# Seven-product down projections for the first parts of all half layers

## The chip, the cores and the metric

The kernel runs on one core of a Trainium2 chip. A core has TensorE (PE in the profile; its weight loads are listed as PEld), VectorE (DVE), ScalarE (ACT), GpSimd (POOL) and SyncE (SP); the last three also issue DMAs, and DMAs that add to their destination go through POOL's queue. The metric is the device time of one execution in microseconds, lower is better; shown is the median of the runs of a kernel.

## The reference

One inference step of a decoder with two layers on 512 prompt positions and 8 sample positions, 1024 channels. Each layer does x += 0.5 * SwiGLU(rms(x)), then a mixer, then a second half SwiGLU. So there are four "half layers" with their own weights:

```python
def _swiglu(x, wg, wu, wd):
    return (jax.nn.silu(x @ wg) * (x @ wu)) @ wd
...
x = x + 0.5 * _swiglu(_rmsnorm(x, norm_g[l, 0]), ffn_w_gate[l, 0], ffn_w_up[l, 0], ffn_w_down[l, 0])
```

`wg` and `wu` are 1024 x 2816, `wd` is 2816 x 1024. The mixer of layer 0 is a causal pooling over windows of 2 to 16 positions, that of layer 1 a windowed attention with sinks; neither is touched by the change. Outputs are the two final activations and the states.

## The kernel before

All activations lie transposed, channels on partitions, in tiles of 128 x 520: the 520 columns are the tokens (512 and 8), and they are worked in two halves of `H` = 260. Every float32 product is made of three products of float32r operands: a tensor is split into a high part (a rounded copy, made by ScalarE, names ending in `h`) and a low part (the rest, made by VectorE, names ending in `l`), and high x high, low x high and high x low are added in PSUM (`terms`). Weights are split the same way into `wh` (L260) and `wl` (L261), in pieces of 128 x 4 x 128, from loaded chunks `raw`.

A half layer (`ffn`, index `fi` from 0 to 3) has 22 tiles of 128 hidden channels, cut into `PARTS` of 8, 8 and 6. For each part it first makes the hidden tiles (gate and up products, silu, their product), then the down projection of that part, which is added to x.

- **Hidden tiles.** The first `NPL[fi]` (4, 3, 2, 3) tiles of a half layer are plain (`plain_tile`): they need only x, since the sums of inputs for the other form are being made meanwhile (`sums`, L783 to L791, fed in by `hooks`), and the norm factor R is not known yet. All others use a seven-product form (`strassen_tile`): gate and up, upper and lower half of the channels, and the two halves of the tokens make 2 x 2 blocks, and seven products of sums of blocks replace eight. The sums on the side of x are the tiles `tt` (names `th`, `tl`). The sums on the side of the weights are made by accumulating DMAs on POOL's queue (L191, L192) and by VectorE (L197, L201); the tile `S` has four buffers.
- **Which operands are free.** The plain tiles read both token halves of all tiles of x (`mov`). The seven-product tiles don't read the second token half of the first four.
- **Down projection.** In the plain form (L815 to L851) each of 8 output tiles takes its 8 or 6 hidden tiles times three terms times two token halves. In the seven-product form (`strassen_down`, L718) pairs of output tiles are made of seven products; it wants sums of hidden tiles, which `HiddenSums` makes as the hidden tiles come: for every two of them B11 (a split of half a tile), T1, T2, B21, B22, T3 and T4. B11 is put where it needs no room of its own: in the second token half of `mov[k]` (L606), which nobody reads any more. Before the change only the second part of each half layer is in `SEVEN` (L33) and has this form; the others use `Hidden`, one split for each hidden tile.

`Weights` holds the order of chunks and pieces: `plan_ffn` writes for each part which chunks are loaded and which pieces are split, in the order of use, and up to five pieces (`ahead`) are split before TensorE gets to them. Chunks have three buffers. A scheduler that simulates the program with its own costs orders the instructions of each engine, except where `later` pins them; so a change in one place can move instructions of all engines nearby. PSUM is handed out in four pairs of banks (`duo`), so that two seven-product tiles can be under way.

At the end of a part in seven-product form its last product is left open and is made inside the next tile (`unfinished`, `finish`).

Of the kernel before, what the change touches and what calls it, by code (L numbers as in the profile page):

```python
# [11 lines left out]
F32 = mybir.dt.float32  # L12
F32R = mybir.dt.float32r
I32 = mybir.dt.int32
AF = mybir.ActivationFunctionType
ALU = mybir.AluOpType
AX = mybir.AxisListType

P = 128
# [5 lines left out]
TOK = SP + NS  # L25
# [4 lines left out]

FIRST = 264
NPL = (4, 3, 2, 3)
SEVEN = {(0, 1), (1, 1), (2, 1), (3, 1)}  # L33
HD = 64
NB = SP // P
WINS = (2, 4, 8, 16)
# [244 lines left out]
def yoco_step(ctx, tc, ins, outs):  # L281
    nc = tc.nc
# [3 lines left out]
    V, S, T = nc.vector, nc.scalar, nc.tensor  # L286
# [16 lines left out]
    def pair(tags, shape, dtype=F32R):  # L303

        return tuple(big.tile(shape, dtype, tag=t, name=t) for t in tags)
# [9 lines left out]
    def split(dst, src, scale=None):  # L315

        hi, lo = dst
        if scale is None:
            S.activation(hi, src, AF.Copy)  # L319
            V.tensor_tensor(lo, src, hi.bitcast(F32), op=ALU.subtract)  # L320
        else:
            S.activation(hi, src, AF.Copy, scale=scale)
            V.scalar_tensor_tensor(lo, src, scale, hi.bitcast(F32), op0=ALU.mult, op1=ALU.subtract)
# [9 lines left out]
    def ld(dst, src):  # L333
        return lambda raw: later(nc.sync.dma_start(dst(raw), src))
# [22 lines left out]
    def plan_ffn(l, f):  # L357
# [4 lines left out]
        for pi, n in enumerate(PARTS):  # L362
            for j in range(t0, t0 + n):
# [13 lines left out]
                else:  # L377
                    W.sums(ch, ld(lambda t: t, u3[:, :4, c]))
            if (2 * l + f, pi) in SEVEN:
                tiles = []  # L380
# [36 lines left out]
    for t in range(0, 8, 2):  # L417
        gp, i = t // 4, t % 4
# [3 lines left out]
                    lambda raw, e=e: raw.rearrange("p k (e i d) -> p k e i d", e=2, i=2)[:, :, e],  # L422
# [12 lines left out]
    for g in range(2):  # L435
        for c in range(2):
# [4 lines left out]
                        lambda raw, e=e: half(raw)[e * 64 : (e + 1) * 64],  # L441
# [28 lines left out]
    def hcols(t, hf):  # L470
        return t[:, hf * H : (hf + 1) * H]
# [14 lines left out]
    nu = [2]  # L486
# [88 lines left out]
    class Hidden(list):  # L575


        def __init__(self, tags):
            self.tags = tags

        def take(self, g):
            hp = pair(self.tags, [P, TOK])
            split(hp, g)
            self.append(hp)

    class HiddenSums:


        def __init__(self, tmp, mov, tags, n):
            self.tmp, self.mov, self.tags, self.n = tmp, mov, tags, n  # L590
            self.b = {q: [] for q in ("B11", "T1", "T2", "B21", "B22", "T3", "T4")}
            self.even = None

# [9 lines left out]
        def take(self, g):  # L603
            k = len(self.b["T3"])
            if self.even is None:
                b11 = tuple(hcols(z, 1) for z in self.mov[k])  # L606
                split(b11, hcols(g, 0))
                self.b["B11"].append(b11)
                t12 = self.tmp.tile([P, TOK], F32, tag="u", name="t12", bufs=nu[0])
                t1 = hcols(t12, 0)  # L610
                V.tensor_tensor(t1, hcols(g, 0), hcols(g, 1), op=ALU.subtract)
                z = pair(self.tags, [P, TOK])
                self.both(z, "T1", "T2")
                if 2 * k + 2 == self.n:
                    split(tuple(hcols(a, 0) for a in z), t1)
                self.even = g, t12, z
                return
            (e, t12, z), self.even = self.even, None
            t1, t2 = hcols(t12, 0), hcols(t12, 1)
            t34 = self.tmp.tile([P, TOK], F32, tag="u", name="t34", bufs=nu[0])  # L620
            t3, t4 = hcols(t34, 0), hcols(t34, 1)
            V.scalar_tensor_tensor(t2, t1, -1.0, hcols(g, 1), op0=ALU.mult, op1=ALU.subtract)
            if 2 * k + 2 == self.n:
                split(tuple(hcols(a, 1) for a in z), t2)
            else:
                split(z, t12)
            w = pair(self.tags, [P, TOK])
            self.both(w, "B21", "B22")
            split(w, g)
            V.tensor_tensor(t3, hcols(g, 1), hcols(e, 1), op=ALU.subtract)  # L630
            V.scalar_tensor_tensor(t4, t2, -1.0, hcols(g, 0), op0=ALU.mult, op1=ALU.subtract)
            v = self.more(k)
            self.both(v, "T3", "T4")
            split(v, t34)
# [159 lines left out]
    def ffn(fi, tmp, mov, hooks, tt, tags, after, before_last=None, first=None, by_parts=None, hold=False):  # L794

        j = 0
        for pi, n in enumerate(PARTS):
            last = pi == len(PARTS) - 1
            seven = (fi, pi) in SEVEN
            hs = HiddenSums(tmp, mov, tags, n) if seven else Hidden(tags)  # L800
            for _ in range(n):
                if j == 0 and first is not None:
                    plain_end(tmp, *first, hs)
# [90 lines left out]
    with ff_pool() as tmp:  # L894
# [132 lines left out]

        after = deferred(1, tmp, "g", XX, mov1, TW, True)
        ffn(0, tmp, mov0, start_hooks(tmp, 0, tt, 2), tt, HH, after, pool_prep(), first, hold=True)

    with tc.tile_pool(name="pm", bufs=2, reuse_waits="tile") as pm:
# [133 lines left out]
    with ff_pool() as tmp:  # L1165
# [112 lines left out]
        step = lambda: next(steps, None)  # L1278
        hooks = [step, outputs] + [step] * 4
        ffn(2, tmp, mov3, hooks, tt, XX, deferred(4, tmp, "g", HH, mov4), attention_prep())  # L1280


# [586 lines left out]
```

## Time and profile before

| | us |
|---|---|
| median of 3 runs (lowest, highest) | 1665.18 (1664.43, 1668.25) |
| the profiled execution | 1663.9 |
| its span, from first to last instruction | 1661.8 |
| TensorE busy | 1633.8 (98% of the span) |
| VectorE busy | 1329.6 (80%) |
| ScalarE busy | 931.6 (56%) |
| POOL busy | 196.5 (12%) |
| mean granted TensorE clock | 0.995 |

How to read the rows: L with a number is a line of the kernel. "ps<-th,wh" says that the tile ps is written from th and wh. In groups, "x704 | 469.2, 688 | 127.4 <-ACT wh L260 125.1" means 704 instructions, 469.2 us busy, 688 ns mean of one, 127.4 us idle time of the engine before them, most of it ended by ScalarE's instruction on L260 that writes wh. In a timeline the columns are start, duration, engine, line, operation, tiles, shapes; idle time before it stands in brackets. In a list of waits the numbers are total us, times, longest. Instructions of one engine overlap a little: a VectorE instruction of 0.70 us can be followed by the next 0.60 us after its start, and busy time counts the overlap once.

The half layers begin (first matmuls of the first part) at about 9, 403, 794 and 1294 us; their second parts run from 151.7 to 270.3, 539.2 to 657.6, 913.3 to 1031.7 and 1429.2 to 1547.9.

### The profile page before, as it was taken

The page shows a single profiled execution, that of the slowest core. Times are in us where ns is not written, and L with a number is a line of the kernel's source. Part 1 is how long each engine was busy: PE and PEld are TensorE (multiplying, and loading weights), DVE is VectorE, ACT ScalarE, POOL GpSimd, SP SyncE. Part 2 cuts the span into 40 slices and gives each one's busy share as a digit, 9 for nine tenths or more (in the row PEclk, how much of TensorE's full clock was granted, in tenths as well). Part 3 has the DMA queues.
Part 4 walks back from the last instruction along what each step waited for, and adds up shares of the span by engine and source line. Part 5 has one row for each costly group of instructions (what it writes and reads, how often), then busy time and mean ns, then how long its engine had stood idle before and what let it go on. Part 6 is the DMA issues. An engine that isn't in the chain of part 4 may idle for free.

```text
span 1661.8 us, 34718 instructions
## 1 busy us (share of the span) xinstructions
PE 1633.8 (98%) x13578; PEld 1621.9 (98%) x13578; DVE 1329.6 (80%) x2589; ACT 931.6 (56%) x1900; POOL 196.5 (12%) x262
## 2 busy tenths in 40 slices
PE   9999999999999999999999999999989999999997
PEld 9999999999999999999999999999989999999996
DVE  6866999877875899888775899886787785799876
ACT  5643665556652665555552665555785653465554
POOL 0101111000101111100201111101210100111100
PEclk9999999999999999999999999999999999999999
DMA  8545778752555778744756787753222555577741
GB/s 222 124 136 130 174 178 180 183 157 91 123 157 134 165 176 180 165 134 107 185 149 134 162 178 182 166 179 97 57 52 77 134 139 141 131 176 181 176 130 52
DMA packets 345712, 240.69 MB, mean 145 GB/s; under 512 B 11438, under 2 KB 316326, under 8 KB 345508
## 3 DMA queue, kind: packets, MB, share of 16 engines
q1 hardware_dynamic: 313790, 183.10, 39.7%
q0 software_dynamic: 28000, 50.28, 18.6%
q10 hardware_dynamic: 3758, 5.09, 1.0%
q8 instruction: 107, 1.75, 0.5%
q14 instruction: 57, 0.47, 0.1%
HBM read 185.56 MB, written 6.11 MB: 115 GB/s over the span
## 4 chain that ended last, share of the span: by engine, by line
PE 92%; ACT 3%; DVE 2%; issue 1%; DMA 1%; POOL 0%; ACTq 0%; DVEq 0%; POOLq 0%
PE ps L563 55%; PE ps L535 31%; DMA pr<-in_bands_dram 1%; PE ps L1077 1%; PE ps L1455 1%; ACT sm L1399 1%; PE ps L1052 0%; PE ps L1424 0%; ACT xh L319 0%; PE ps L494 0%; PE ps L1743 0%; DVE wl L261 0%; PE ps L1368 0%; ACT wh L260 0%; PE ps L932 0%
## 5 line engine op out<-in xcount | busy, mean ns | idle before, releaser
L260 ACT ACTIVATE wh<-raw 128x512 fp32r<-128x512 f32 (+1 forms) x762 | 452.0, 620 | 394.1 <-PE ps L535 197.4
L261 DVE TENSOR_TENSOR wl<-raw,wh 128x512 fp32r<-128x512 f32 (+1 forms) x762 | 501.0, 678 | 136.4 <-ACT wh L260 133.7
L563 PE MATMUL ps<-th,wh 128*128 128x260 f32 x1216 | 344.0, 284 | 1.2 <-ACT sa L701 0.9
L563 PE MATMUL ps<-tl,wh 128*128 128x260 f32 x1216 | 342.6, 282 | 0.0
L563 PE MATMUL ps<-th,wl 128*128 128x260 f32 x1216 | 341.2, 283 | 0.2 <-DVE wl L261 0.2
L563 PEld LDWEIGHTS ps<-th,wh 128*128 128x128 f32 x1216 | 228.7, 188 | 2.8 <-ACT sa L701 1.1
L563 PEld LDWEIGHTS ps<-tl,wh 128*128 128x128 f32 x1216 | 229.0, 188 | 0.0
L563 PEld LDWEIGHTS ps<-th,wl 128*128 128x128 f32 x1216 | 227.9, 188 | 0.4 <-DVE wl L261 0.4
L563 PE MATMUL ps<-xh,wh 128*128 128x260 f32 x784 | 220.9, 283 | 0.7 <-ACT sb L698 0.7
L563 PE MATMUL ps<-xl,wh 128*128 128x260 f32 x784 | 220.3, 282 | 0.0
L563 PE MATMUL ps<-xh,wl 128*128 128x260 f32 x784 | 218.7, 282 | 0.0
L192 POOL DMA_DIRECT2D raw<-raw x92 | 79.3, 862 | 1148.1 <-DVE wl L261 421.1
L535 PE MATMUL ps<-hh,wh 128*128 128x260 f32 x956 | 193.4, 284 | 0.6 <-ACT vtok L1236 0.6
L535 PE MATMUL ps<-hl,wh 128*128 128x260 f32 x956 | 193.2, 282 | 0.0
L535 PE MATMUL ps<-hh,wl 128*128 128x260 f32 x956 | 192.1, 282 | 0.0
L563 PEld LDWEIGHTS ps<-xh,wh 128*128 128x128 f32 x784 | 147.3, 188 | 1.3 <-ACT sb L698 1.3
L535 PEld LDWEIGHTS ps<-hh,wh 128*128 128x128 f32 x956 | 146.8, 188 | 1.5 <-ACT vtok L1236 0.9
L535 PEld LDWEIGHTS ps<-hl,wh 128*128 128x128 f32 x956 | 147.7, 188 | 0.0
L563 PEld LDWEIGHTS ps<-xl,wh 128*128 128x128 f32 x784 | 147.5, 188 | 0.0
L535 PEld LDWEIGHTS ps<-hh,wl 128*128 128x128 f32 x956 | 147.3, 188 | 0.0
L563 PEld LDWEIGHTS ps<-xh,wl 128*128 128x128 f32 x784 | 146.9, 189 | 0.0
L563 PE MATMUL ps<-hl,wh 128*128 128x260 f32 x448 | 125.8, 282 | 0.0
(329 smaller groups left out, 3391.1 us busy)
## 6 DMA issues: line engine op xcount, KB each, us to landing
raw<-in_ffn_w_gate_dram SPq DMA_DIRECT2D x87, 512.0 KB, 4.6
raw<-in_ffn_w_up_dram SPq DMA_DIRECT2D x87, 512.0 KB, 5.8
raw<-raw POOLq DMA_DIRECT2D x92, 256.0 KB, 3.4
S<-raw POOLq DMA_DIRECT2D x92, 256.0 KB, 4.5
S<-in_ffn_w_up_dram SPq DMA_DIRECT2D x76, 256.0 KB, 5.6
raw<-in_ffn_w_down_dram SPq DMA_DIRECT2D x16, 1024.0 KB, 5.4
raw<-in_ffn_w_down_dram SPq DMA_DIRECT2D x64, 256.0 KB, 4.6
raw<-in_ffn_w_down_dram SPq DMA_DIRECT2D x16, 768.0 KB, 4.3
```

The lines of the kernel that those rows point to most:

```text
L192: G.dma_start(blk(raw, 2, 1), blk(raw, 1, 1), accum_op=ALU.add)
L260: pin(nc.scalar.activation(dh, src, AF.Copy))
L261: pin(nc.vector.tensor_tensor(dl, src, dh.bitcast(F32), op=ALU.subtract))
L535: ins = T.matmul(banks[:, hf, :H], a[:, kk, :], hcols(b, hf), start=(first and i == 0), stop=(last and i == 2),)
L563: T.matmul(bank[:, :H], a[:, kk, :], b, start=(not more and kk == 0 and i == 0), stop=(kk == 3 and i == 2), skip_group_check=more,)
L1077: T.matmul(po[:, half * 256 : half * 256 + 256], z[:, tau, c], b, start=(i == 0), stop=(i == len(lst) - 1),)
L1399: S.activation(z, z, AF.Exp, scale=-1.0, bias=nm[:, i : i + 1], accum_out=self.den[:, i : i + 1])
L1455: T.matmul(po[:, bi * 256 : (bi + 1) * 256], a, p_[:, kc_], start=(n == 0), stop=(n == 3 * len(kts) - 1),)
```

## The change

The first parts (8 tiles) of all four half layers go into `SEVEN` as well, so all parts but the third have the seven-product down. In a first part the early hidden tiles come while plain tiles still read both halves of `mov`. So as long as that is so, `HiddenSums` puts B11 into a spare pair (`kept`, of the buffers `ph` and `pl`, which T3 and T4 use too), two halves to a pair, and when the plain tiles are done it copies them by DMAs on POOL's queue to their place in `mov` and gives the spare pair back: four DMAs in the first half layer, two in each other. `plain` tells the class how many plain tiles there are (0 for second parts).

The other edit concerns the sums. T1 and T2 had a tile of their own (`t12`); now T1 is made in place of the first half of the even hidden tile, and T2 in place of its second half. T3 needs that second half, so it is made before T2, and it stands at another place in the order.

```diff
-SEVEN = {(0, 1), (1, 1), (2, 1), (3, 1)}
+SEVEN = {(f, p) for f in range(4) for p in (0, 1)}
...
-        def __init__(self, tmp, mov, tags, n):
+        def __init__(self, tmp, mov, tags, n, plain):
             self.tmp, self.mov, self.tags, self.n = tmp, mov, tags, n
+            self.plain, self.kept = plain, None
...
             k = len(self.b["T3"])
             if self.even is None:
                 b11 = tuple(hcols(z, 1) for z in self.mov[k])
+                self.b["B11"].append(b11)
+                if 2 * k < self.plain - 1:
+                    if self.kept is None:
+                        self.kept = tuple(self.tmp.tile([P, TOK], F32R, tag=q, name=q, bufs=3) for q in ("ph", "pl"))
+                    b11 = tuple(hcols(z, k) for z in self.kept)
+                elif self.kept is not None:
+                    for i in range(k):
+                        for z, c in zip(self.mov[i], self.kept):
+                            nc.gpsimd.dma_start(hcols(z, 1), hcols(c, i))
+                    self.kept = None
                 split(b11, hcols(g, 0))
-                self.b["B11"].append(b11)
-                t12 = self.tmp.tile([P, TOK], F32, tag="u", name="t12", bufs=nu[0])
-                t1 = hcols(t12, 0)
-                V.tensor_tensor(t1, hcols(g, 0), hcols(g, 1), op=ALU.subtract)
+                t1 = hcols(g, 0)
+                V.tensor_tensor(t1, t1, hcols(g, 1), op=ALU.subtract)
                 z = pair(self.tags, [P, TOK])
                 self.both(z, "T1", "T2")
                 if 2 * k + 2 == self.n:
                     split(tuple(hcols(a, 0) for a in z), t1)
-                self.even = g, t12, z
+                self.even = g, z
                 return
-            (e, t12, z), self.even = self.even, None
-            t1, t2 = hcols(t12, 0), hcols(t12, 1)
+            (e, z), self.even = self.even, None
+            t1, t2 = hcols(e, 0), hcols(e, 1)
             t34 = self.tmp.tile([P, TOK], F32, tag="u", name="t34", bufs=nu[0])
             t3, t4 = hcols(t34, 0), hcols(t34, 1)
+            V.tensor_tensor(t3, hcols(g, 1), t2, op=ALU.subtract)
             V.scalar_tensor_tensor(t2, t1, -1.0, hcols(g, 1), op0=ALU.mult, op1=ALU.subtract)
             if 2 * k + 2 == self.n:
                 split(tuple(hcols(a, 1) for a in z), t2)
             else:
-                split(z, t12)
+                split(z, e)
             w = pair(self.tags, [P, TOK])
             self.both(w, "B21", "B22")
             split(w, g)
-            V.tensor_tensor(t3, hcols(g, 1), hcols(e, 1), op=ALU.subtract)
             V.scalar_tensor_tensor(t4, t2, -1.0, hcols(g, 0), op0=ALU.mult, op1=ALU.subtract)
...
-            hs = HiddenSums(tmp, mov, tags, n) if seven else Hidden(tags)
+            hs = HiddenSums(tmp, mov, tags, n, NPL[fi] if pi == 0 else 0) if seven else Hidden(tags)
```

## The prediction

> **What bounds the kernel now.** I read the page first: engine shares, then the chain that ended last. Then stretches of time by stage, then TensorE's list of waits, and last the order of single instructions where the change lands.
>
> ```profile
> PE 1633.8 (98%) x13578; PEld 1621.9 (98%) x13578; DVE 1329.6 (80%) x2589; ACT 931.6 (56%) x1900; POOL 196.5 (12%) x262
> ...
> PE 92%; ACT 3%; DVE 2%; issue 1%; DMA 1%; POOL 0%; ACTq 0%; DVEq 0%; POOLq 0%
> ```
>
> TensorE is busy 98% of the span and makes up 92% of the chain. VectorE, at 80%, is the runner-up. A matmul taken away is therefore worth its time wherever VectorE can follow. The stretches tell where it can. Columns: the stretch, its length, then busy us (instructions) of PE, PEld, DVE, ACT, POOL, then clock and DMA.
>
> ```profile
> core 0: us, PE busy (x) PEld busy (x) DVE busy (x) ACT busy (x) POOL busy (x), PEclk, DMA share, GB/s
> 49.00:151.70 102.70, 102.70 (x860) 102.70 (x859) 73.85 (x128) 48.05 (x88) 8.69 (x10) 1.00 0.53 131
> 427.20:539.20 112.00, 111.71 (x929) 111.15 (x929) 80.34 (x138) 52.12 (x96) 10.45 (x12) 1.00 0.55 134
> 793.00:913.30 120.30, 120.13 (x1002) 120.13 (x1003) 81.53 (x135) 53.86 (x100) 17.17 (x23) 1.00 0.62 151
> 1311.00:1429.20 118.20, 118.20 (x988) 118.20 (x987) 83.83 (x143) 55.53 (x100) 10.44 (x12) 1.00 0.53 130
> 151.70:270.30 118.60, 118.36 (x985) 117.95 (x984) 108.66 (x201) 70.17 (x144) 19.09 (x22) 1.00 0.75 170
> ...
> 107.70:151.70 44.00, 44.00 (x371) 44.00 (x370) 23.16 (x36) 11.20 (x19) 5.21 (x6) 1.00 0.55 126
> 495.20:539.20 44.00, 44.00 (x371) 44.00 (x370) 23.03 (x36) 11.18 (x18) 5.23 (x6) 1.00 0.56 126
> ...
> 228.00:270.30 42.30, 42.30 (x356) 42.30 (x355) 41.10 (x76) 23.35 (x49) 6.91 (x8) 1.00 0.76 173
> 615.50:657.60 42.10, 42.10 (x354) 42.10 (x353) 40.90 (x75) 23.05 (x48) 6.91 (x8) 1.00 0.73 171
> ```
>
> The first four rows are the first parts of the four half layers, from about where the norm is known to the end of their down projection. The fifth is a second part, which has the seven-product down already: VectorE is busy 108.66 of 118.60 us there and TensorE still loses only 0.24. The last four rows set a plain down (VectorE 23 of 44 us) beside a seven-product down (41 of 42): that stage runs with VectorE nearly full, and TensorE does not stop. A matmul costs 44.00 us / 371 = 0.119 us.
>
> ```profile
> PE ps L563 <- ACT sa L701: 0.9, 1, 0.9
> ...
> PE ps L563 <- DVE wl L261: 0.2, 1, 0.2
> ```
>
> In its list of waits TensorE has waited for a weight's low half once, for 0.2 us. So before the change nothing in these parts is left to win but matmuls.
>
> **The change, part by part.**
>
> *Matmuls.* A plain down of a part of 8 hidden tiles is 8 outputs x 8 x 3 terms x 2 halves = 384 matmuls of 260 columns. The seven-product form is 4 pairs x 7 products x 4 x 3 = 336. Four parts lose 48 each: 192 x 0.119 = 22.8 us, all on the path. [...]
>
> *VectorE.* Durations and starts differ, so I price it by starts.
>
> ```profile
> 63.63 0.43 DVE L789 SCALAR_TENSOR_TENSOR t<-t,xb 128x260 f32<-128x260 f32 x1
> 63.97 0.70 DVE L675 SCALAR_TENSOR_TENSOR g<-ps,t 128x520 f32<-128x520 f32 x1
> 64.58 0.70 DVE L320 TENSOR_TENSOR tl<-t,th 128x520 fp32r<-128x520 f32 x1
> 65.18 0.70 DVE L261 TENSOR_TENSOR wl<-raw,wh 128x512 fp32r<-128x512 f32 x1
> 65.78 0.71 DVE L320 TENSOR_TENSOR tl<-t,th 128x520 fp32r<-128x520 f32 x1
> 66.39 0.70 DVE L261 TENSOR_TENSOR wl<-raw,wh 128x512 fp32r<-128x512 f32 x1
> ```
>
> Busy, it begins a full-width instruction (512 or 520) every 0.605 us (63.97 to 66.39 is four), a half-width one (260) every 0.34. One part gains, full width: 28 low halves of weights (L261) and 8 sums (L197, L201), 11 splits in the hidden sums, 16 in the down's evacuation. Half width: 22 in the hidden sums, 12 in the down. It loses 16 low halves, 8 splits of hidden tiles, and 16 of the add (L823, L824). Net 23 full and 34 half: 23 x 0.605 + 34 x 0.34 = 25.4 us, 102 for the four. The work between the down's products stands beside matmuls as in the 228.00 row, so in the sum it costs nothing while VectorE keeps up. If that cover goes, what is late is a low half that TensorE needs, or an evacuation that frees a PSUM pair.
>
> Does it keep up? After the change the four stretches hold 73.85 + 25.4 = 99.2, 105.7, 106.9 and 109.2 us of VectorE work. TensorE's own time for them is 5.7 us (48 x 0.119) shorter: 97.0, 106.3, 114.6 and 112.5. The first is over by 2.2 and the second just fits. The low halves of weights run up to five pieces ahead of TensorE, 5 x 12 x 0.119 = 7 us, so some of the overhang can slide into the second part, which has 118.60 - 108.66 = 10 us of room.
>
> *The tight place* is where plain tiles end and seven-product tiles begin. VectorE owes there the sums of the inputs (L783 to L789 and their splits), the first weight sums, and now also the hidden sums of the plain tiles. I counted VectorE's queue in the built order of the changed kernel from an anchor that both orders share, against TensorE's position.
>
> ```profile
> 48.99 0.69 DVE L261 TENSOR_TENSOR wl<-raw,wh 128x512 fp32r<-128x512 f32 x1
> ...
> 427.21 0.69 DVE L261 TENSOR_TENSOR wl<-raw,wh 128x512 fp32r<-128x512 f32 x1
> ...
> 1317.88 0.69 DVE L261 TENSOR_TENSOR wl<-raw,wh 128x512 fp32r<-128x512 f32 x1
> ```
>
> ```profile
> 63.47 0.28 PE L563 MATMUL ps<-xh,wh 128*128 128x260 f32 x1
> ...
> 439.91 0.28 PE L563 MATMUL ps<-xh,wh 128*128 128x260 f32 x1
> ...
> 1330.64 0.28 PE L563 MATMUL ps<-xh,wh 128*128 128x260 f32 x1
> ```
>
> The second fence has the first matmul of the first seven-product tile in half layers 1, 2 and 4. The method holds on the old order: from 48.99, 20 full and 12 half give 16.2 us, so the fourth input's split ends at 65.2; the row that begins at 64.58 ends at 65.28. In the new order of half layer 1 the worst is the low half of the next tile's second weight: 24 full and 21 half, 21.7 us, ready at 70.7. TensorE wants it 46 matmuls after 63.47, at 68.9, because the new order puts the next tile's first product ahead of the late inputs. Lost: 1.8 us. Half layer 2: 21 full and 15 half, 17.8, ready at 445.0; wanted 35 matmuls on, at 444.1. Lost: 0.9. Half layer 4: the fourth input is 16 full and 11 half, 13.4, ready at 1331.3; wanted 24 matmuls on, at 1333.5: nothing lost. Half layer 3 makes its input sums before the norm, and its order of matmuls at this place is unchanged: nothing. Beside that I allow 1 us for VectorE's extra round trips to ScalarE. Bounds: 0 (they hide, as in the fifth stretch) to 8 us (the idle share of that stretch everywhere, the slower rival below); I take 1, near the first, since the fifth stretch does the same work.
>
> *ScalarE* gets, per part, 15 more full and 18 more half instructions.
>
> ```profile
> L261 DVE TENSOR_TENSOR wl<-raw,wh 128x512 fp32r<-128x512 f32 x704 | 469.2, 688 | 127.4 <-ACT wh L260 125.1
> L260 ACT ACTIVATE wh<-raw 128x512 fp32r<-128x512 f32 x704 | 422.4, 628 | 357.4 <-PE ps L535 180.6 <-PE ps L563 91.0 <-DVE raw L197 48.4
> ...
> L192 POOL DMA_DIRECT2D raw<-raw x92 | 79.3, 862 | 1148.1 <-DVE wl L261 421.1 <-DMA raw<-in_ffn_w_up_dram 209.1 <-DVE t L784 84.1
> ...
> L727 ACT COPY sa<-ps 128x260 f32<-128x260 f32 x16 | 5.9, 366 | 8.7 <-PE ps L563 8.7
> ```
>
> 15 x 0.63 + 18 x 0.37 = 16 us on 48 to 56 in stretches of over 97: no bound.
>
> *The spare pair and POOL.* Ten moves of half tiles (4, 2, 2, 2) are new on POOL's queue, as are 8 accumulating DMAs per part, each some 0.86 us of issue (L192). A move waits until TensorE has read the plain tiles' operand for the last time, so the next tile's weight sums stand behind it. In half layer 1 that is the third seven-product tile:
>
> ```profile
> 56.07 0.85 POOL L192 DMA_DIRECT2D raw<-raw  x1 [10.88 <-DVE g L675]
> ```
>
> ```profile
> 77.07 0.68 DVE L197 TENSOR_TENSOR raw<-raw,S 128x512 f32<-128x512 f32 x1
> ```
>
> It went out at 56.07, before the plain tiles' end at 63.47. The move's operand is free half a plain tile (48 matmuls, 5.7 us) before that end, at 57.8; with four moves the sums go out by 62. VectorE adds to the landed tile at 77.07 (L197), and the tile's own turn comes two tiles (168 matmuls, 20 us) after 63.47, at 83.5. Slack over 10 us: cost nothing.
>
> *SP and memory.* 20 loads in place of 4 per part, in runs half as long. The DMA share should go from 0.55 toward the 0.76 of the 228.00 row, where TensorE lost nothing: no cost.
>
> *Sums in place.* The tile that held the first two sums is gone wherever hidden sums are made: no instruction is saved, and the difference now follows its split on VectorE, which was in order anyway: nothing.
>
> **Sum.** -22.8 + 1.8 + 0.9 + 1.0 = -19.1 us. The profiled execution took 1663.9 (span 1661.8 and 2.1 around it), 1.3 under the median 1665.18. 1663.9 - 19.1 + 1.3 = 1646.
>
> **The rivals.**
>
> *VectorE binds the first parts at the share that it reaches in a seven-product down,* 0.97 (40.90 of 42.10). The four would take 99.2/0.97 = 102.3, 109.0, 114.6 (TensorE) and 112.6: -0.4, -3.0, -5.7, -5.6, together -14.7, or 1650. For it: the 99.2 against 97.0; against: pieces made ahead.
>
> *A VectorE instruction costs its duration, not the distance of starts.* The rows give 0.70 and 0.43: 23 x 0.70 + 34 x 0.43 = 30.7 per part. Over TensorE's time by 7.6, 4.7, 0 and 2.0: 14.3 of the 22.8 are lost, 1657. Against it stand the six rows above, which overlap. [...]
>
> *Slower: VectorE needs the idle it has in the second part.* There it is busy 108.66/118.60 = 0.916, the rest mostly waits on ScalarE's high halves (125.1 us of the 127.4 before L261, over the whole program). If that share is the most it can do among tiles, the four parts take 108.3, 115.4, 116.7 and 119.2: +5.6, +3.4, -3.6, +1.0, together +6.4: 1672. It decides from a share of 421/453.2 = 0.93 down (all work over the present length). Against it: TensorE set the pace there, so the idle may be slack; and 0.97 is seen in the down.
>
> *The moves hold up POOL.* If each of the four in half layer 1 waits for the plain end and for the one before it to land (3 to 4 us), the next sums land near 63.5 + 4 x 4.5 + 4 = 85, some 2 us after their turn at 83.5, and less with two moves elsewhere: 1648 to 1652.
>
> **How the numbers follow.** Forecast 0.58 (own range 1641 to 1649), the 0.97 share 0.16, durations 0.05, POOL 0.04: all faster, 0.83. No change (gain and loss cancel at a share near 0.93) 0.05. Slower 0.12. The range 1641 to 1655 takes in the full 22.8 and the first and last of these rivals and leaves out some 0.2. A measurement of this kernel tells about 0.2%, 3.3 us, from no change.
>
> **What would show it.** Right: 192 fewer 128x260 matmuls; the four stretches 4 to 6 us shorter with VectorE at 93 to 97%; TensorE waits for low halves (L261, L320) of 1 to 2 us only near 66 to 72 and 444 to 447; second and third parts as long as before. Wrong: such waits spread over the tiles and the down of the first parts, PSUM waits on VectorE's evacuations, or POOL's weight sums (L191, L192) landing late behind the moves.

## The result, and the profile after

| | before | changed |
|---|---|---|
| median of 4 runs each (lowest, highest), us | 1664.81 (1664.39, 1668.25) | 1654.46 (1654.14, 1657.26) |
| the profiled execution, us (its span) | 1663.9 (1661.8) | 1657.3 (1655.5) |

The changed kernel takes 0.9937 of the time before, 95% interval 0.9920 to 0.9954: some 10 us faster, where 19 were forecast. Timed once more beside other kernels (c1 below) it came to 0.9921, 0.9896 to 0.9946. The profiled execution is the slowest of the four; why is told below.

The page of the changed kernel, shares of engines and chain:

```profile
PE 1624.3 (98%) x13386; PEld 1607.8 (97%) x13386; DVE 1421.8 (86%) x2817; ACT 980.1 (59%) x2032; POOL 228.9 (14%) x304
...
PE 90%; DVE 3%; ACT 3%; DMA 1%; issue 1%; POOL 0%; SPq 0%; DVEq 0%; ACTq 0%; POOLq 0%
```

192 matmuls are gone, 13578 to 13386, as forecast. But TensorE's part of the chain fell from 92 to 90%; VectorE's rose from 2 to 3%, and ScalarE's stayed at 3%. The list of waits of the changed kernel says at what (total us, times, longest):

```profile
PE ps L563 <- ACT wh L260: 3.8, 6, 0.8
PE ps L563 <- ACT sb L707: 1.8, 2, 1.4
...
PE ps L563 <- ACT sa L744: 1.3, 2, 0.7
...
PE ps L563 <- DVE wl L261: 1.0, 2, 0.6
```

Before, this form of matmul waited 0.9 us each for two of ScalarE's copies (sa once; sb four times, 0.2 at most), 0.3 for VectorE's sb and 0.2 for a low half, and no wait for a high half stood in the list:

```profile
PE ps L563 <- ACT sb L698: 0.9, 4, 0.2
```

Now ScalarE's high halves (L260) and copies (L707, L744) stand first, and VectorE's low halves only behind them.

Stretches of the changed kernel, columns as in the prediction: the four first parts, from the same places as before (they took 102.70, 112.00, 120.30 and 118.20 us); the four second parts, from the end of the first part's down on; the first seven-product tiles of half layer 1; the attention stage, and a piece of it.

```profile
core 0: us, PE busy (x) PEld busy (x) DVE busy (x) ACT busy (x) POOL busy (x), PEclk, DMA share, GB/s
48.40:150.30 101.90, 99.41 (x812) 97.79 (x811) 95.63 (x180) 61.39 (x122) 16.04 (x20) 1.00 0.69 161
425.40:534.30 108.90, 106.87 (x881) 105.78 (x881) 101.00 (x190) 63.46 (x128) 16.69 (x20) 1.00 0.70 157
790.60:906.00 115.40, 114.96 (x954) 114.44 (x955) 102.85 (x188) 65.55 (x133) 22.93 (x31) 1.00 0.79 181
1311.90:1425.30 113.40, 112.92 (x940) 112.50 (x940) 104.63 (x196) 66.68 (x132) 16.71 (x20) 1.00 0.69 158
...
148.20:270.30 122.10, 121.39 (x1011) 120.98 (x1010) 113.15 (x210) 71.66 (x145) 20.80 (x24) 1.00 0.81 179
532.20:656.20 124.00, 122.29 (x1010) 120.99 (x1009) 113.74 (x211) 71.20 (x146) 20.80 (x24) 1.00 0.81 183
903.90:1027.70 123.80, 121.95 (x1010) 121.08 (x1010) 113.21 (x210) 71.81 (x145) 20.81 (x24) 1.00 0.79 176
1423.30:1545.50 122.20, 121.92 (x1009) 121.14 (x1009) 112.18 (x209) 69.82 (x145) 20.83 (x24) 1.00 0.78 178
...
49.00:75.00 26.00, 23.84 (x189) 22.84 (x188) 25.13 (x50) 19.03 (x37) 3.96 (x6) 1.00 0.41 97
1121.50:1331.60 210.10, 203.24 (x1677) 198.12 (x1676) 156.51 (x433) 135.15 (x338) 29.19 (x56) 0.94 0.34 83
1226.90:1240.50 13.60, 13.60 (x69) 13.15 (x69) 8.25 (x36) 6.39 (x26) 3.17 (x4) 0.50 0.24 55
```

The first parts are 0.8, 3.1, 4.9 and 4.8 us shorter where 5.7 was to be had: half layers 3 and 4 got nearly all, 2 half, 1 almost nothing. The second parts, whose code only had its sums put in place, took longer. Between the same places (the stretches of the sections above begin 2 us later and end 1 earlier) they took, before the change:

```profile
149.60:271.30 121.70, 121.46 (x1011) 121.05 (x1010) 111.57 (x204) 71.68 (x145) 19.09 (x22) 1.00 0.74 167
537.10:658.60 121.50, 121.26 (x1010) 120.84 (x1009) 111.47 (x204) 71.54 (x145) 19.04 (x22) 1.00 0.72 167
911.30:1032.70 121.40, 121.16 (x1010) 120.74 (x1010) 111.46 (x204) 71.48 (x145) 19.06 (x22) 1.00 0.77 170
1427.10:1548.90 121.80, 121.56 (x1011) 121.14 (x1010) 111.54 (x204) 71.56 (x145) 19.08 (x22) 1.00 0.75 169
```

For exact lengths I count matmuls along TensorE, which the change leaves countable: 84 to a seven-product tile, 384 or 336 to a down. "First part" runs from the first seven-product matmul to the end of that down, "second part" over the 1008 matmuls behind it. All kernels, in us, half layers 1 to 4:

| | first parts | second parts | ratio to before (95%) |
|---|---|---|---|
| before | 86.1, 97.2, 106.5, 96.5 | 121.7, 121.5, 121.4, 121.7 | 1 |
| changed | 85.3, 94.1, 101.5, 91.7 | 122.1, 124.1, 123.8, 122.3 | 0.9937 (0.9920-0.9954) |
| c1 changed again | 85.0, 94.1, 101.7, 91.5 | 122.4, 123.9, 122.1, 122.1 | 0.9921 (0.9896-0.9946) |
| b1 in place only | 86.1, 97.2, 106.5, 96.5 | 121.2, 121.0, 120.9, 121.2 | 0.9996 (0.9986-1.0007) |
| b2 own tile in second | 84.6, 94.1, 101.0, 92.1 | 122.1, 122.4, 122.0, 122.1 | 0.9909 (0.9890-0.9927) |
| b3 own where possible | 84.1, 94.3, 101.2, 91.2 | 121.9, 121.9, 121.8, 122.1 | 0.9904 (0.9886-0.9922) |
| b4 no plain sums | 80.5, 90.8, 101.0, 90.9 | 121.1, 123.5, 122.5, 122.5 | 0.9891 (0.9862-0.9919) |
| c2 first down closed | 86.1, 94.1, 101.9, 91.5 | 121.6, 121.3, 121.5, 122.2 | 0.9878 (0.9863-0.9894) |
| c3 half layers 3, 4 | 86.1, 97.2, 103.4, 92.2 | 121.2, 121.0, 121.9, 122.5 | 0.9914 (0.9896-0.9931) |
| c4 moves on SP | 84.6, 94.1, 101.0, 91.5 | 122.1, 124.3, 124.1, 121.2 | 0.9913 (0.9892-0.9933) |
| d1 no second S | 85.6, 94.0, 101.9, 91.5 | 122.1, 123.6, 123.0, 121.2 | 0.9904 (0.9879-0.9929) |
| d2 more plain tiles | 81.9, 91.9, 101.2, 91.2 | 121.9, 121.7, 121.8, 122.1 | 0.9866 (0.9842-0.9890) |
| d3 sums on GpSimd | 83.9, 97.5, 106.2, 91.8 | 122.1, 121.9, 121.8, 122.2 | 0.9926 (0.9898-0.9954) |
| e1 own in last pair | 81.9, 91.9, 100.6, 91.0 | 121.6, 121.2, 121.3, 121.6 | 0.9830 (0.9812-0.9847) |

(In d2 and e1 the first two numbers include the added plain tile, 96 x 0.119 = 11.4 us, so that they compare.) The stages of one kernel repeat within 0.3 us from profile to profile, apart from the second part of half layer 3 (123.8 and 122.1). The total repeats worse, since it also has the attention stage in it (210.1 us in the changed kernel, 203.9 in c1).

The account of the two profiled executions, span against span, is then: first parts -13.8 (-22.8 and 9.0 lost), second parts +5.9, third parts -1.0, the stages between +5.7, nearly all of it attention (204.3 to 210.1), and behind the last matmul -3.1 (12.6 to 9.5). Together -6.3, the difference of the spans.

### The profile page after: what moved, and what is told of

Same layout as the page of the kernel before. It is cut to its first block, busy times and chain, and to the rows that moved or that the text cites. A ratio compares the mean times of both kernels' runs of the same rounds, so it can differ in the third digit from the quotient of the medians.

```text
span 1655.5 us, 34978 instructions
## 1 busy us (share of the span) xinstructions
PE 1624.3 (98%) x13386; PEld 1607.8 (97%) x13386; DVE 1421.8 (86%) x2817; ACT 980.1 (59%) x2032; POOL 228.9 (14%) x304
## 4 chain that ended last, share of the span: by engine, by line
PE 90%; DVE 3%; ACT 3%; DMA 1%; issue 1%; POOL 0%; SPq 0%; DVEq 0%; ACTq 0%; POOLq 0%
PE ps L563 64%; PE ps L535 20%; ACT wh L260 1%; DVE wl L261 1%; PE ps L1464 1%; PE ps L1061 1%; DMA pr<-in_bands_dram 1%; PE ps L1086 1%; ACT sm L1408 1%; PE ps L1377 0%; PE ps L1433 0%; PE ps L494 0%; PE ps L1752 0%; PE ps L1759 0%; DMA raw<-in_ffn_w_gate_dram 0%
## 5 line engine op out<-in xcount | busy, mean ns | idle before, releaser
L260 ACT ACTIVATE wh<-raw 128x512 fp32r<-128x512 f32 (+1 forms) x794 | 465.3, 619 | 262.7 <-PE ps L535 81.3
L261 DVE TENSOR_TENSOR wl<-raw,wh 128x512 fp32r<-128x512 f32 (+1 forms) x794 | 518.0, 675 | 71.1 <-ACT wh L260 69.1
L563 PE MATMUL ps<-th,wh 128*128 128x260 f32 x1216 | 343.7, 284 | 1.5 <-ACT wh L260 1.2
L563 PE MATMUL ps<-th,wl 128*128 128x260 f32 x1216 | 342.4, 282 | 0.6 <-DVE wl L261 0.6
L563 PE MATMUL ps<-tl,wh 128*128 128x260 f32 x1216 | 342.3, 282 | 0.0
L563 PE MATMUL ps<-xh,wh 128*128 128x260 f32 x896 | 253.6, 284 | 3.3 <-ACT sb L707 1.8
L563 PE MATMUL ps<-xl,wh 128*128 128x260 f32 x896 | 251.6, 282 | 0.0
L563 PE MATMUL ps<-xh,wl 128*128 128x260 f32 x896 | 250.5, 282 | 0.5 <-DVE wl L261 0.4
L563 PEld LDWEIGHTS ps<-th,wh 128*128 128x128 f32 x1216 | 228.4, 188 | 3.7 <-ACT wh L260 2.5
L563 PEld LDWEIGHTS ps<-th,wl 128*128 128x128 f32 x1216 | 228.8, 188 | 0.8 <-DVE wl L261 0.8
L563 PEld LDWEIGHTS ps<-tl,wh 128*128 128x128 f32 x1216 | 229.0, 188 | 0.0
L563 PE MATMUL ps<-hh,wh 128*128 128x260 f32 x656 | 184.7, 285 | 2.4 <-ACT wh L260 1.8
L563 PE MATMUL ps<-hl,wh 128*128 128x260 f32 x656 | 183.8, 283 | 0.2 <-DVE hl L320 0.2
L563 PE MATMUL ps<-hh,wl 128*128 128x260 f32 x656 | 183.1, 282 | 0.0
L563 PEld LDWEIGHTS ps<-xh,wh 128*128 128x128 f32 x896 | 168.3, 188 | 5.3 <-ACT sb L707 2.2
L563 PEld LDWEIGHTS ps<-xh,wl 128*128 128x128 f32 x896 | 168.1, 188 | 0.9 <-DVE wl L261 0.9
L563 PEld LDWEIGHTS ps<-xl,wh 128*128 128x128 f32 x896 | 168.4, 188 | 0.0
L563 PEld LDWEIGHTS ps<-hh,wh 128*128 128x128 f32 x656 | 123.0, 188 | 4.3 <-ACT wh L260 2.8
L563 PEld LDWEIGHTS ps<-hl,wh 128*128 128x128 f32 x656 | 123.3, 188 | 0.4 <-DVE hl L320 0.4
L563 PEld LDWEIGHTS ps<-hh,wl 128*128 128x128 f32 x656 | 123.0, 188 | 0.0
L535 PE MATMUL ps<-hh,wh 128*128 128x260 f32 x572 | 116.3, 285 | 0.6 <-ACT vtok L1245 0.6
```

The lines of the kernel that those rows point to most:

```text
L260: pin(nc.scalar.activation(dh, src, AF.Copy))
L261: pin(nc.vector.tensor_tensor(dl, src, dh.bitcast(F32), op=ALU.subtract))
L535: ins = T.matmul(banks[:, hf, :H], a[:, kk, :], hcols(b, hf), start=(first and i == 0), stop=(last and i == 2),)
L563: T.matmul(bank[:, :H], a[:, kk, :], b, start=(not more and kk == 0 and i == 0), stop=(kk == 3 and i == 2), skip_group_check=more,)
```

## The experiments

**b1, sums in place alone.** `SEVEN` as before the change, `HiddenSums` as after it.

```diff
-SEVEN = {(f, p) for f in range(4) for p in (0, 1)}
+SEVEN = {(0, 1), (1, 1), (2, 1), (3, 1)}
```

> The kernel before with one edit of the two: sums in place, while the first parts keep their plain down. Theory A (the second parts' down projections became 0.9, 2.3, 2.8 and 1.4 us longer, 7.4 in all, because T1 in place has to wait for the split of the same half tile, is put late, and the down's first operands are late with it): the same four stages are longer here too, about 7 us in all, and the time is near 1664.8 + 7 = 1672. Theory B (they became longer because the first parts' new VectorE work, or the order that it brings, reaches into the second parts): nothing is seen here, 1664 to 1666.

Theory A fell: 0.9996, and the second parts became 0.5 us shorter each, not longer. In place is harmless, even good, as long as the first parts are plain.

**b2, a tile of their own for the sums of second parts; b3, for all pairs without a plain tile.**

```diff
-                t1 = hcols(g, 0)
+                t12 = g if self.plain else self.tmp.tile([P, TOK], F32, tag="u", name="t12", bufs=nu[0])
+                t1 = hcols(t12, 0)
```

(T2 and T3 follow as before the change; in b3 the condition is `2 * k < self.plain`.)

> The changed kernel with sums in place in the first parts only; the second parts have the tile of their own back. Theory A: the second parts' down projections are back at 40.2 to 40.3 us, 7.4 us are won, about 1654.2 - 7.4 = 1647. Theory B: still 41.2 to 43.0 us, 1654.

> As the run before, but in the first parts too the sums are in place only for pairs that hold a plain tile; all other pairs have the tile of their own. Theory A: also the 0.5 to 0.9 us that TensorE loses at the head of each of the first parts' downs (2.5 us in all) go, about 1645. Theory B: as the changed kernel, 1654. If the two second tiles that are held press on the two buffers of u, the tiles of the first parts get longer instead.

The downs of the second parts came back to 40.2 to 40.3 us in b2, as theory A said; but their tiles grew to 81.8 to 82.2 (80.6 to 81.5 in the changed kernel, 81.3 to 81.4 before), so only 1.5 to 2 us are won in half layers 2 and 3 (in 3 nothing, if c1's 122.1 below is the measure) and nothing in 1 and 4. With b1 this means that the downs' loss needs both edits together. A loss in the tiles remains: the second parts of b2 are still 2.4 us over those before the change in all, those of b3 1.4. b3 also wins 1 us in the first downs. Both kernels' ratios, 0.991 and 0.990, lie within the interval that c1 gave for the changed kernel: the stages show more than the total time can.

**b4, the plain tiles' sums left out.**

```diff
+            if 2 * k < self.plain - 1:
+                ...
+                    for q in self.b:
+                        self.b[q].append(None)
+                return
```

> The changed kernel without the hidden sums of the pairs that are wholly plain tiles (two pairs in the first half layer, one in each other): their splits, sums and moves are left out, and the down takes the operands of a later pair in their place, so the result isn't the reference's; the matmuls are the same. Theory C (the 3.6 and 2.1 us that the first parts' tiles of half layers 1 and 2 got longer are these sums, which queue on VectorE and ScalarE with the input sums and weights at the first seven-product tiles): both go to under 0.5 us each, 1654.2 - 5 = 1649. Rival D (what is late there are the evacuations and the new order of products, with or without the sums): both stay, 1653 to 1654. Rival E (the moves on POOL hold up the weight sums): the time goes as in C, but with waits on low halves of sums (L197, L201) two tiles later and not at the first tiles.

Theory C holds. The tiles of the first parts of half layers 1 and 2 took 40.3 and 50.2 us (43.8 and 53.4 in the changed kernel, 40.3 and 51.3 before). The stretch that TensorE lost 2.16 us in, in this kernel:

```profile
49.00:75.00 26.00, 26.00 (x219) 26.00 (x218) 22.44 (x42) 16.31 (x30) 1.73 (x2) 1.00 0.50 122
```

VectorE is at 22.44 of 26 us in place of 25.13, and TensorE does not stop. Waits on low halves of sums two tiles later (rival E) were not there. The second parts of half layers 2 to 4 stayed long, so that loss is another one.

How sums that belong to finished tiles stop TensorE is seen in ScalarE's timeline of the changed kernel. Ahead of the dots is the loss at 71.8 us, behind them the head of the second part's down in half layer 2:

```profile
69.30 0.37 ACT L705 COPY sa<-ps 128x260 f32<-128x260 f32 x1
71.50 0.63 ACT L260 ACTIVATE wh<-raw 128x512 fp32r<-128x512 f32 x1 [1.83 <-PE ps L563]
72.03 1.15 ACT L319 ACTIVATE hh<-g 128x520 fp32r<-128x520 f32 x2
73.09 0.35 ACT L707 COPY sb<-ps 128x260 f32<-128x260 f32 x1
...
613.90 0.63 ACT L260 ACTIVATE wh<-S 128x512 fp32r<-128x512 f32 x1 [2.04 <-DVE wl L261]
614.44 0.61 ACT L260 ACTIVATE wh<-raw 128x512 fp32r<-128x512 f32 x1
616.11 0.64 ACT L260 ACTIVATE wh<-raw 128x512 fp32r<-128x512 f32 x1 [1.06 <-issue]
616.65 0.63 ACT L736 COPY sa<-ps 128x260 f32<-128x260 f32 x2
617.17 0.65 ACT L715 ACTIVATE t<-g 128x520 f32<-128x520 f32 x1
617.78 0.42 ACT L319 ACTIVATE hh<-g 128x260 fp32r<-128x260 f32 x1
619.06 0.64 ACT L319 ACTIVATE hh<-g 128x520 fp32r<-128x520 f32 x1 [0.86 <-DVE g L722]
620.06 1.67 ACT L260 ACTIVATE wh<-raw 128x512 fp32r<-128x512 f32 x3 [0.36 <-DVE raw L201]
621.64 0.35 ACT L738 COPY sb<-ps 128x260 f32<-128x260 f32 x1
```

The copy of sb, which frees a PSUM bank that TensorE needs, stands in ScalarE's queue behind a weight split that waits 1.83 us for TensorE, and then behind two splits of hidden sums (1.15 us). TensorE stands still for 1.4 us until that copy is done. ScalarE is idle 41% of the span, but this copy ran only when the three splits ahead of it were done. In the second stretch the split of the hidden tile (hh from 128x520) waits 0.86 us for VectorE's evacuation (L722) with the weights of the next products behind it; TensorE loses 0.8 us to that high half at 621.8.

**c1, the changed kernel once more, unaltered.**

> The changed kernel once more, unaltered. In its first profile the attention stage between half layers 3 and 4, which the change doesn't touch, took 210.1 us against 204.3 before, with TensorE at half its clock from 1213 to 1220 and from 1227 to 1240. Theory G (where the half-clock stretches fall differs from run to run): here they fall elsewhere or are fewer, the stage takes another time between 204 and 210, and the other stages repeat within 0.3 us. Rival (they come with the changed kernel): 210 again with the same stretches. The median of the runs stays within 1653 to 1656.

Theory G holds for the clock. The attention stage in c1's profile:

```profile
1120.90:1324.80 203.90, 193.14 (x1676) 187.79 (x1675) 156.51 (x433) 134.94 (x338) 29.30 (x56) 1.00 0.35 85
```

203.9 us at clock 1.00, where the first profile had 210.10 at 0.94: the same instructions. That 6 us of the first profile is no effect of the change. The span was 1648.2, the median of the runs 1651.9 (1648.7 to 1661.0), a little below what was expected. Half layer 3's second part was 122.1 this time, so its loss is partly a matter of the execution.

**c2, the first down closed before the second part begins.**

```diff
                 strassen_down(tmp, hs)
+                if pi == 0:
+                    finish()
                 continue
```

(The order of weight pieces stays as it was, so the closing product and the next tile's first two take each other's weights; the number and kind of all instructions are the same.)

> The changed kernel with one edit: the first parts' down closes its last product itself, in place of leaving it open until the second part's first tile. Sums in place alone did not lengthen the second parts (tiles and down together 121.2, 121.0, 120.9 and 121.2 us, against 122.1, 124.1, 123.8 and 122.3 in the changed kernel); so the loss needs both edits. Theory H (the open product carries the first part into the order of the second): all four are back at 120.9 to 121.2, 6 us are won there, and each closing costs TensorE 1 to 2 us in its place, so about 1654 - 6 + 6 = 1654 by the clock but with the stages so. Rival I (the order of the second part comes out otherwise whatever is handed over): at least two of the four stay over 122 us.

Second parts of 121.6, 121.3, 121.5 and 122.2: half layers 2 and 3 are back within 0.7 us of b1, 1 half way, 4 not. The gain is large only in half layer 2 (123.9 to 124.1 without the edit); in 3 it is 0.6 or 2.3 us, by the execution that it is set against. So the open product does carry the first part into the order of the second (H) there, not in half layer 4, and closing cost some 1 us in half layer 1 and nothing that shows in the others, instead of 1 to 2. Its interval, 0.9863 to 0.9894, ends just below c1's from the same comparison.

**c3, half layers 3 and 4 only; c4, the moves on SP's queue.**

```diff
+SEVEN = {(0, 1), (1, 1), (2, 0), (2, 1), (3, 0), (3, 1)}
```

```diff
-                            nc.gpsimd.dma_start(hcols(z, 1), hcols(c, i))
+                            nc.sync.dma_start(hcols(z, 1).bitcast(F32), hcols(c, i).bitcast(F32))
```

> The changed kernel with seven-product first parts in half layers 3 and 4 only. By the stages of the changed kernel's trace, half layer 3 is worth 0 - 5.0 - 0.4 + 2.8 = -2.7 us and half layer 4 -0.1 - 4.7 - 0.8 + 1.4 = -4.3, and the sums in place alone -0.5 in each of the other two: about 1664.8 - 8 = 1657. Theory J (a second part is longer where its own half layer's first part is in the new form): the second parts of half layers 1 and 2 take 121.2 and 121.0 us as with sums in place alone, those of 3 and 4 take 123.8 and 122.3. Rival: other lengths in half layers 3 and 4, although nothing of their own code differs from the changed kernel, which would say that their order hangs on what came long before.

> The changed kernel with the ten moves of the spare pair on SP's queue in place of POOL's. Theory C (the plain tiles' sums on VectorE and ScalarE make the loss at the first seven-product tiles, and the moves cost nothing): the tiles of the first parts of half layers 1 and 2 stay at 43.8 and 53.4 us and the time at 1654. Rival E (the moves hold up POOL's weight sums): these stages get 2 us or more shorter, 1650 to 1652. If instead the moves hold up the loads that stand behind them on SP, the same tiles get longer.

c3: half layers 1 and 2 are exactly b1's, and half layer 4 is about the changed kernel's, as theory J said; half layer 3's second part was 121.9, where 123.8 was expected, near c1's 122.1, and its first part 103.4, 1.9 longer, although nothing of its own code differs: there the rival holds, and the order hangs on what came long before. With 0.9914 it is no slower than the changed kernel: the new first parts of half layers 1 and 2 win 0.8 and 3.1 us and cost 0.9 and 3.1 in the second parts behind them, as against b1. c4: the tiles stay at 43.8 and 53.4 us, so rival E is out a second time; the moves cost nothing on either queue.

**d1, no late sum in the second parts' downs.** In the changed kernel ScalarE's 2.04 us at 613.90 above are a wait for S, which an accumulating DMA issued at 609.67 makes (the row names wl L261; at the same place in c1 ScalarE waits 2.61 us, put down to the DMA S<-raw). It looked like the cause.

```diff
-            G.dma_start(s1, blk(raw, 2, 2), accum_op=ALU.add)
+            if not bare:
+                G.dma_start(s1, blk(raw, 2, 2), accum_op=ALU.add)
```

> The changed kernel, but in the downs of the second parts the second of the four chunks leaves out the accumulating DMA that makes its sum S; S holds the loaded weights alone, so the result isn't the reference's. In the traces ScalarE stands still before it splits this S for 0 to 0.4 us before the change, 0.1 to 1.8 with sums in place alone, and 0.7 to 2.9 in the changed kernel, with everything behind it in its queue. Theory L (that late sum is what lengthens the second parts): S is there some 4 us earlier, ScalarE does not wait for it, tiles and down of the second parts together take 121.0 to 121.3 us in place of 122.1 to 124.1, and 5 to 6 us are won against the changed kernel: a ratio of 0.989. Rival M (the order of the hidden tile's evacuation and of T1 in place is enough by itself): at least half layers 2 and 3 stay over 122.5 us.

The wait is gone (ScalarE splits that S without standing idle in all four), and the second parts still take 122.1, 123.6, 123.0 and 121.2. Theory L fell except perhaps for half layer 4, which varies by as much without it (121.2 in c4); M holds. The loss is not in this DMA; what is left is the order at the end of the part.

That order is seen beside ScalarE's timeline of b1 at the same place, with nearly the same order of products on TensorE:

```profile
618.27 0.36 ACT L736 COPY sa<-ps 128x260 f32<-128x260 f32 x1
618.52 0.42 ACT L319 ACTIVATE hh<-g 128x260 fp32r<-128x260 f32 x1
619.23 0.38 ACT L736 COPY sa<-ps 128x260 f32<-128x260 f32 x1 [0.28 <-PE ps L563]
619.50 0.64 ACT L715 ACTIVATE t<-g 128x520 f32<-128x520 f32 x1
622.09 0.38 ACT L738 COPY sb<-ps 128x260 f32<-128x260 f32 x1 [1.95 <-PE ps L563]
622.37 0.64 ACT L319 ACTIVATE hh<-g 128x520 fp32r<-128x520 f32 x1
```

In b1 the split of the first sum (hh from 128x260) comes ahead of the second copy of sa and of the silu (L715), and the split of the full hidden tile stands behind the copy of sb. In the changed kernel it is the other way round: two copies, silu, split, and the full split, with three weight splits, ahead of sb.

**d2, one plain tile more in half layers 1 and 2; d3, sums on GpSimd.** Both on the base of b3.

```diff
-NPL = (4, 3, 2, 3)
+NPL = (5, 4, 2, 3)
```

```diff
-                V.tensor_tensor(t1, hcols(g, 0), hcols(g, 1), op=ALU.subtract)
+                (nc.gpsimd if 2 * k < self.plain - 1 else V).tensor_tensor(t1, hcols(g, 0), hcols(g, 1), op=ALU.subtract)
```

(and the same for T3 of those pairs, and for T1 and T3 of the input sums with k > 1)

> As b3 (a tile of their own for the sums of all pairs without a plain tile), with one plain tile more in half layers 1 and 2 (5, 4, 2, 3). A plain tile has 96 matmuls, a seven-product tile 84: 12 x 0.119 = 1.4 us more in each. Theory C (VectorE is short where plain tiles end; it is busy 25.1 of the 26 us from 49 to 75 in the changed kernel and 22.4 where the plain tiles' sums are left out): a longer lead relieves it, the waits at the first seven-product tiles (about 2.9 and 2.7 us in the list of matmuls that start late) go under 1 us each, and the kernel is 1 to 3 us faster than b3, a ratio near 0.989. Rival N (one more plain tile brings its own hidden sums, so the shortage only comes later): the waits stay and the kernel is 3 us slower than b3.

> As b3, with the subtractions T1 and T3 of the wholly plain pairs and of the last two pairs of input sums on GpSimd in place of VectorE: 8 half-width instructions of 0.34 us in half layer 1, 6 in the others, 2.7 and 2.0 us off VectorE where plain tiles end. Theory C: the waits there shrink by about as much, from 2.9 and 2.7 us to under 1 each, ratio near 0.988. Rival O (GpSimd takes about 1 us for such an instruction, 956 ns for the 128x256 one in this trace, behind DMA issues of 0.86 us, so the input sums come later): the waits at the first seven-product tiles grow, in half layers 3 and 4 too, where there were none.

d2: 0.9866, so 6 us better than b3 by the ratios and more than the 1 to 3 expected. No matmul at the first seven-product tiles starts late any more (of the waits of L563 in the whole program, those with the largest total come to 1.1 us, five for copies of sb, 0.2 at most), and the first parts are 2.2 and 2.4 us shorter although 12 matmuls were added to each. d3: rival O. Three of the four groups of moved sums on GpSimd in this kernel (count, busy us and mean ns; the fourth, T3 of the hidden sums, has 953):

```profile
L796 POOL TENSOR_TENSOR t<-xa 128x260 f32<-128x260 f32 x8 | 7.6, 950 | 6.0 <-ACT xa L791 3.4 <-DVE tl L320 2.4 <-DVE t L802 0.2
L621 POOL TENSOR_TENSOR g<-g 128x260 f32<-128x260 f32 x5 | 6.8, 1365 | 4.7 <-DVE pl L320 4.3 <-PE ps L535 0.4
L801 POOL TENSOR_TENSOR t<-xb,xa 128x260 f32<-128x260 f32 x8 | 6.7, 836 | 10.7 <-DVE pl L320 8.3 <-DVE tl L320 2.4
```

So 836 to 1365 ns each, against 0.42 us for the same sums on VectorE in the changed kernel (L620, L631, L792, L797: 421 to 424 ns) and 0.34 between its starts: two to three times the duration. Half layers 2 and 3 lose 3 and 5 us against b3. Not all of that is waiting: in this profile TensorE's granted clock was 0.50 from 446.1 to 449.5 and from 811.3 to 814.7, inside these two stages, where its matmuls start about 0.1 us later each, some 1.5 us in each stage. Whether the waits just before brought that on was not tried.

**e1, sums in place but for the last pair of each part,** with d2's plain tiles.

```diff
+                t12 = g if 2 * k + 2 < self.n else self.tmp.tile([P, TOK], F32, tag="u", name="t12", bufs=nu[0])
```

> As d2 (5, 4, 2, 3 plain tiles), but sums in place for all pairs of hidden tiles except the last pair of each part, which has the tile of its own. In b3 and d2 the second parts (tiles and down together) take 121.7 to 122.1 us: nothing is lost in the down, but the tiles lose some 0.4 us twice to the copy of sb (L707 of the changed kernel). With sums in place alone they took 120.9 to 121.2; in the changed kernel 122.1 to 124.1. Theory P (the loss is made by T1 in place of the last pair, next to the down that wants it, and the gain by the other pairs in place): 121.0 to 121.3 in all four, 2 to 3 us faster than d2, a ratio of 0.985. Rival (the last pair is not the place): two or more of the four over 122.

Second parts of 121.2 to 121.6, none over 122: theory P, with 0.3 less than hoped in half layers 1 and 4. As against the kernel before the change, their tiles are 0.8 to 1.0 us shorter and their downs 0.6 to 0.9 longer (40.8 to 41.2): the downs' loss is smaller, not nothing, and the tiles make up for it. The ratio is 0.9830 (0.9812 to 0.9847), median 1637.8 us over 5 runs: faster than both kernels. Its page:

```profile
PE 1613.8 (99%) x13410; PEld 1602.2 (98%) x13410; DVE 1414.0 (86%) x2801; ACT 973.0 (60%) x2020; POOL 226.4 (14%) x302
```

## Why the prediction was right or wrong

The direction was right, and 1654.5 lies just inside the range (1641 to 1655), but outside the forecast's own one (1641 to 1649). About half of the gain forecast came, and some of it from places that the forecast did not name: 3.1 us lie behind the last matmul. Without them the median would lie outside the range, so that it lies inside is luck.

- *Matmuls, -22.8.* Right: 192 fewer, and where nothing is late they still start every 0.119 us.
- *"Lost: 1.8 us. Half layer 2: ... Lost: 0.9."* The right places (65.7 to 71.8, 440.7 to 447.6) and the right cause, shown by b4 and d2, but mis-sized: the tiles there got 3.55 and 2.05 us longer, 5.6 in place of 2.7. I had counted VectorE's queue alone; of TensorE's waits in the list above, only 1.0 us is for low halves. The longest single stop, 1.4 us in half layer 1, is a copy in ScalarE's queue (shown above), and "ScalarE ... no bound" was said of its share of busy time, which says nothing about what stands ahead of what. Half layers 3 and 4: nothing forecast, nothing lost.
- *The allowance of 1.0 for round trips.* The first downs lost 3.5 us: they took 41.5, 40.7, 41.2 and 41.3 us against 336 x 0.119 = 40.0, while the plain ones were 1.2 over their matmuls' time in all. The stretch that I took the 1 us from, a whole second part, lost 0.24 us, and its down alone 0.2 to 0.3 over 40.0. b3 has 40.3 to 41.0, so part of it is the in-place sums; the cause of the rest was not found.
- *"Second and third parts as long as before"* and *"Sums in place ... nothing."* The step that failed. Taken alone, in place does cost nothing (b1), and the seven-product first parts with a tile of their own in the second leave the downs there as they were, though not their tiles (b2). Together they cost 5.9 us in the second parts in the first profile and 4.2 in c1. I had argued about one dependence on VectorE; what changed is the order that the scheduler makes of a part's end, where T1 of the last pair can come only after the split of the same half tile. e1 shows the place: with a tile for that pair alone the second parts take 0.5 us less in all than before the change (with in place alone, b1, it was 2.0 less). c2 points to the open product as the way from the first part into the second, clearly in half layer 2 only. Which single instruction tips the order was not tried, so the cause is shown to its place and no further.
- *POOL, SP, memory.* Right. DMA shares are 0.69 to 0.79 in the first parts, and c4 shows the moves free; in the changed kernel they landed 2.6 us after their issue (median of L616, 5.7 at most). The late S in the second parts is real and nearly without effect (d1).
- *The rival with VectorE at a share of 0.97* gives -0.4, -3.0, -5.7, -5.6 for the first parts, measured -0.8, -3.1, -5.0, -4.8 (by counted matmuls). Its numbers fit better than the forecast's, its mechanism does not: VectorE was busy 0.89 to 0.94 of those stretches, and d2 loses nothing in the first tiles with as many hidden sums. The work was late in one place, not too much overall. *Durations price* and *slower*: VectorE's work in the four stretches was 404 us, under the 421 that I had counted by starts, and over the whole span its busy time grew by 92.2 us (1329.6 to 1421.8), where starts gave 102 and durations 123.

The sum with the measured terms: -22.8 + 5.6 + 3.5 + 4.2 to 5.9 = -9.5 to -7.8, where the prediction had -19.1. The medians show -10.4 and the ratio of c1 some -13; the remaining few us are in the third parts (-1.0), in stages that the change doesn't touch and behind the last matmul (-3.1).

## What to carry to other kernels

Here the matmuls taken away were won where the operands were early (5.0 and 4.8 of 5.7 us in half layers 3 and 4), and partly lost where one form of work hands over to another (3.55 and 2.05 us in the tiles of half layers 1 and 2); so walk the queue of every engine through that place in order, ScalarE's copies of PSUM included, and not only the engine with the highest share. Where a scheduler orders the instructions, an edit that adds a dependence can be free alone and cost several us beside another edit (sums in place: the second parts 2.0 us shorter in b1, 4.2 to 5.9 longer in the changed kernel): compare the lengths of stages that should not have changed, by counting matmuls, before trusting the total. One cheap, plain tile more as a lead (d2, 0.9866) was worth more than sums moved to an idle engine (d3, 0.9926; both on b3's 0.9904).

## What the runs showed of the hardware

TensorE's clock went to half in the attention stage in stretches that differ from execution to execution of one program: 13.6 us from 1226.9 (clock 0.50 in the row above) in one profile of the changed kernel, none within that stage in the other, and the stage took 210.1 and 203.9 us. In the profiles before and after the change the stretches at half clock up to the last matmul last 3.4, 6.8 or 13.6 us; all but one (3.4 from 373.6 in the changed kernel) lie in the attention stage. There they come to 10.2 us before the change (3.4 from 1197.4, 6.8 from 1217.9; the stage took 204.3 us) and to 23.8 in the first profile of the changed kernel (3.4 from 1192.8, 6.8 from 1213.2, 13.6 from 1226.9). The longest wait of TensorE in this stage was 1.4 us in both, so the length of a single wait does not decide it here; what does was not shown.

Between the last matmul's start and the end of the span lie 12.6 us before the change and in b1, and 9.5 in both profiles of the changed kernel, with the same instructions. This is 3 us of the difference of the spans. They lie in GpSimd's closing DRAIN: it begins 2.96 us behind the start of the last matmul in all four profiles and takes 8.88 and 8.83 us before the change and in b1, 5.50 and 5.80 in the two of the changed kernel, while SyncE is through its waits for the last stores at 8.7 to 9.0 in all. Every other kernel with first parts in seven-product form has 3.6 to 5.6. GpSimd issues more DMAs in these (244 to 266) than in the two with plain first parts (224); why its DRAIN is shorter was not found.
